# Batched fp32 matmul on one core: loads and stores in one queue, word transposes, full-width matmuls

## The chip, the cores and the metric

The kernel runs on one core of a Trainium2 chip. The metric is device microseconds (us) of one execution, 13 of them for the kernel before. One further execution was taken by the hardware profiler; durations, waits and transfers below come from that one.

## The reference

128 independent products (8 by 16), each of a 256x512 and a 512x384 matrix, in fp32:

```python
b1, b2, m, k, n = 8, 16, 256, 512, 384
return np.matmul(x, weight).astype(np.float32)    # (8, 16, 256, 384)
```

Read are 67.1 MB of `x` and 100.7 MB of `weight`, written are 50.3 MB of output. The kernel casts both inputs to bf16 and sums in fp32.

## The kernel before

One group is two of the 128 matrices (`groups`: 63 pairs, then two single matrices that share one load of `x`). For a group:

- `load_x` (L60) brings the 512 rows of `x` of two matrices, 1 MB, as four consecutive rows per partition, 8 KB in one piece. Partitions 0 to 63 hold the first matrix, 64 to 127 the second. `load_w` (L67) brings one weight matrix, 768 KB, four consecutive rows of K per partition, 6 KB in one piece. Both are issued by SP, in the order x, w, w.
- VectorE (DVE) casts `x` to bf16 in one instruction (L77) and each weight matrix in one (L110).
- TensorE (PE) transposes `x` in 16 blocks of 128x128 bf16 (L82), eight into one PSUM tile; DVE copies each of the two tiles to `x_t` (L86). As the weight rows lie four to a partition, a block takes every fourth column of K (`ko::KO`).
- PE multiplies (L124). A stationary operand is 64 columns of `x_t`, one matrix, so the two matrices of a pair fill the two halves of the output partitions with 32 matmuls of 64 columns by 384. In the two single groups 128 columns are used and 16 matmuls do for one matrix.
- ScalarE (ACT) copies each PSUM tile, 128x768, to `out_sb` (L131), two for a group, and issues the store (L95), 768 KB with 6 KB in one piece per partition. The last two stores are 384 KB with 3 KB per partition.

The code asks for a store three groups late (`LAG`), but the order that the scheduler writes out, and the trace, have each store on ACT's queue right behind its own group's second copy: the first group's copies start at 13.31 and 15.28 us and its store is issued at 16.12 us.

SP's queue has only loads. Buffers: `x_sb` 3, `w_sb` 6, `x_bf` 2, `x_t` 2, `w_bf` 4, `out_sb` 6, PSUM tiles 2 for transposes and 3 for products. Completion counters of transfers are reused in turn, eight in all for loads and stores, four to a group; so each transfer also waits until the one that had its counter, two groups before, has landed.

Of the kernel before, what the change touches and what calls it, by code (L numbers as in the profile page):

```python
# [1 line left out]

# [5 lines left out]


@with_exitstack
def kernel(
    ctx: ExitStack,
    tc: tile.TileContext,
    x: bass.AP,
    weight: bass.AP,
    out: bass.AP,
):
    nc = tc.nc
    P = 128  # L20

    b1, b2, M, K = x.shape
    _, _, _, N = weight.shape
    B = b1 * b2
    KO = K // P

    x_rows = x.rearrange("b1 b2 m k -> (b1 b2 m) k")
    o_rows = out.rearrange("b1 b2 m n -> (b1 b2 m) n")
    w_flat = weight.rearrange("b1 b2 k n -> (b1 b2) k n")

    fp32 = mybir.dt.float32
    bf16 = mybir.dt.bfloat16

    GX = 2
    CX = P // GX
    R = GX * M // P


    groups = [2] * ((B - GX) // 2) + [1] * GX

    LAG = 3

    const = ctx.enter_context(tc.tile_pool(name="const", bufs=1))
    x_pool = ctx.enter_context(tc.tile_pool(name="x_pool", bufs=3))
    xb_pool = ctx.enter_context(tc.tile_pool(name="xb_pool", bufs=2))
    xt_pool = ctx.enter_context(tc.tile_pool(name="xt_pool", bufs=2))
    w_pool = ctx.enter_context(tc.tile_pool(name="w_pool", bufs=6))
    wb_pool = ctx.enter_context(tc.tile_pool(name="wb_pool", bufs=4))  # L50
    out_pool = ctx.enter_context(tc.tile_pool(name="out_pool", bufs=LAG + 3))
    psum_t = ctx.enter_context(tc.tile_pool(name="psum_t", bufs=2, space=bass.MemoryType.PSUM))
    psum_o = ctx.enter_context(tc.tile_pool(name="psum_o", bufs=3, space=bass.MemoryType.PSUM))

    identity = const.tile([P, P], bf16)
    make_identity(nc, identity)

    def load_x(b):
        x_sb = x_pool.tile([P, R, K], fp32, name="x_sb")
        nc.sync.dma_start(  # L60
            x_sb[:], x_rows[b * M : (b + GX) * M].rearrange("(p r) k -> p r k", r=R)
        )
        return x_sb

    def load_w(b):
        w_sb = w_pool.tile([P, KO, N], fp32, name="w_sb")
        nc.sync.dma_start(w_sb[:], w_flat[b].rearrange("(kp ko) n -> kp ko n", ko=KO))  # L67
        return w_sb

    def transpose_x(x_sb, RG):  # L70


        H = R // RG
        x_bf = xb_pool.tile([P, R, K], bf16, name="x_bf")
        x_t = xt_pool.tile([P, RG, KO, P, H], bf16, name="x_t")
        for r0 in range(0, R, 4):
            nc.vector.tensor_copy(out=x_bf[:, r0 : r0 + 4], in_=x_sb[:, r0 : r0 + 4])  # L77
            for r in range(r0, r0 + 4, 2):
                pt = psum_t.tile([P, 2, KO, P], bf16, name="pt")
                for rr in range(2):  # L80
                    for ko in range(KO):
                        nc.tensor.transpose(  # L82
                            pt[:, rr, ko, :], x_bf[:, r + rr, ko::KO], identity
                        )
                j = r % RG
                nc.vector.tensor_copy(  # L86
                    out=x_t[:, j : j + 2, :, :, r // RG], in_=pt[:]
                )
        return x_t

    waiting = []

    def store():
        dram, out_sb = waiting.pop(0)
        nc.scalar.dma_start(out=dram, in_=out_sb)  # L95

    b = 0
    for n, G in enumerate(groups):
        last = n == len(groups) - 1
        C = P // G  # L100
        RG = G * M // P
        if b % GX == 0:
            x_sb = load_x(b)
        w_sb = [load_w(b + i) for i in range(G)]
        if b % GX == 0:
            x_t = transpose_x(x_sb, RG)
        w_bf = []
        for i in range(G):
            t = wb_pool.tile([P, KO, N], bf16, name="w_bf")
            nc.vector.tensor_copy(out=t[:], in_=w_sb[i][:])  # L110
            w_bf.append(t)
        if last:
            while waiting:
                store()

        out_full = out_pool.tile([P, 2 * M // P, N], fp32, name="out_sb")
        out_sb = out_full[:, :RG]
        for r in range(0, RG, 2):
            po = psum_o.tile([P, 2, 512], fp32, name="po")
            for rr in range(2):  # L120
                for ko in range(KO):
                    for i in range(G):
                        c0 = (b % GX + i) * CX
                        nc.tensor.matmul(  # L124
                            po[i * C : (i + 1) * C, rr, :N],
                            x_t[:, r + rr, ko, c0 : c0 + CX, :],
                            w_bf[i][:, ko, :],
                            start=(ko == 0),
                            stop=(ko == KO - 1),
                        )  # L130
            nc.scalar.copy(out=out_sb[:, r : r + 2, :], in_=po[:, :, :N])  # L131
        waiting.append(
            (
                o_rows[b * M : (b + G) * M].rearrange("(p r) n -> p r n", r=RG),
                out_sb,
            )
        )
        if len(waiting) > LAG or last:
            store()
        b += G  # L140


# [1 line left out]
_INS = ['x', 'weight']  # L144
_OUTS = [((8, 16, 256, 384), 'float32')]


# [23 lines left out]
```

## Time and profile before

| | |
|---|---|
| median of 13 runs | 531.51 us (530.08 to 534.75) |
| the profiled execution | 530.08 us |
| its span, first to last instruction | 527.9 us |
| TensorE clock granted, mean | 0.863 |
| busy: PE / DVE / ACT | 342.1 / 277.8 / 103.9 us |
| moved by DMA | 218.59 MB, mean 414 GB/s |

The profiled execution's own time is 2.2 us above its span. "Share" of DMA is the mean busy share of 16 DMA engines; a store or a load is cut over all 16, and counts as landed when the last of them is done. A group passes every 8.1 us (casts of `x` from 5.6 to 515.7 us, 63 steps).

### The profile page before, as it was taken

To read this page: it belongs to the slowest core of one execution; us is meant where nothing else is said; L and a number is where in the kernel's file an instruction comes from. 1 tells how busy PE (TensorE), PEld (TensorE's weight loads), DVE (VectorE), ACT (ScalarE), POOL (GpSimd) and SP (SyncE) were. 2 spreads that over 40 slices of the span, in tenths; PEclk is the share of its full clock that TensorE was granted. 3 is DMA by queue.
4 is the path that set the end of the run, shared out by engine and by line. 5 is a ranking of instruction groups with operands and counts; after the bars stand their busy time and mean duration, and the time that the engine had idled before them with its cause. 6 is when DMAs were issued, how large, how long until landed. Compare 5 with 4: busy or idle time off the path is not lost.

```text
span 527.9 us, 7363 instructions
## 1 busy us (share of the span) xinstructions
PE 342.1 (65%) x3056; PEld 233.1 (44%) x3056; DVE 277.8 (53%) x320; ACT 103.9 (20%) x129; POOL 0.7 (0%) x6
## 2 busy tenths in 40 slices
PE   4685566675764766676657577566676575766764
PEld 2454444444543544444435444344344443544442
DVE  4545545555465544564554545555555555455554
ACT  0212211221211212122112122121111221212212
POOL 0000000000000000000000000000000000000000
PEclk9969888888789878889888878898778988788889
DMA  8999999999999999999999999999999999999994
GB/s 343 405 426 423 425 420 420 425 419 424 422 420 425 421 421 425 421 423 421 423 423 421 421 423 421 423 424 424 422 421 422 422 421 423 421 423 423 424 413 194
DMA packets 37041, 218.59 MB, mean 414 GB/s; under 512 B 4112, under 2 KB 4112, under 8 KB 28816
## 3 DMA queue, kind: packets, MB, share of 16 engines
q1 hardware_dynamic: 27648, 167.78, 76.5%
q10 hardware_dynamic: 9360, 50.34, 23.0%
q8 instruction: 24, 0.39, 0.3%
q14 instruction: 9, 0.07, 0.0%
HBM read 167.77 MB, written 50.33 MB: 413 GB/s over the span
## 4 chain that ended last, share of the span: by engine, by line
DMA 97%; DVE 1%; PE 1%; issue 1%; SPq 0%; ACT 0%; DVEq 0%
DMA x_sb<-in_x_dram 97%; PE po L124 1%; DVE x_t L86 0%; DVE x_bf L77 0%; DVE w_bf L110 0%; SPq L60 0%; SPq L67 0%; ACT out_sb L131 0%; PE pt L82 0%; DVEq L77 0%
## 5 line engine op out<-in xcount | busy, mean ns | idle before, releaser
L124 PE MATMUL po<-w_bf,x_t 128*64 128x384 bf16 (+1 forms) x2032 | 274.7, 405 | 165.0 <-DVE w_bf L110 164.5
L124 PEld LDWEIGHTS <-x_t 128*64 128x64 bf16 (+1 forms) x2032 | 173.0, 134 | 250.9 <-DVE w_bf L110 126.5
L131 ACT COPY out_sb<-po 128x768 f32<-128x768 f32 x128 | 102.6, 802 | 420.0 <-PE po L124 412.5
L77 DVE CAST x_bf<-x_sb 128x2048 bf16<-128x2048 f32 x64 | 78.5, 1227 | 138.8 <-DMA x_sb<-in_x_dram 138.8
L110 DVE CAST w_bf<-w_sb 128x1536 bf16<-128x1536 f32 x128 | 119.9, 955 | 26.9 <-DMA w_sb<-in_weight_dram 26.3
L86 DVE COPY x_t<-pt 128x1024 bf16<-128x1024 bf16 x128 | 83.7, 696 | 78.6 <-PE pt L82 78.6
L82 PE MATMUL pt<-identity,x_bf 128*128 128x128 bf16 x1024 | 70.3, 222 | 16.7 <-DVE x_bf L77 16.7
L82 PEld LDWEIGHTS <-x_bf 128*128 128x128 bf16 x1024 | 60.2, 115 | 39.4 <-DVE x_bf L77 31.0
L131 ACT ACT_TABLE_LOAD x1 | 1.3, 1283 | 0.7 <-PEq L155 0.7
masks.py:199 POOL TENSOR_SCALAR_AFFINE_SELECT identity<-identity 128x128 bf16<-128x128 bf16 x1 | 0.3, 292 | 0.1
masks.py:197 POOL MEMSET identity<- 128x128 bf16 x1 | 0.2, 205 | 0.3 <-POOLq L155 0.3
L155 POOL MEMSET const-bfloat16-1.0<- 128x1 bf16 x1 | 0.1, 101 | 0.0
L155 POOL MEMSET const-uint8-127<- 128x1 uint8 x1 | 0.1, 101 | 0.0
L155 POOL MEMSET const-float32-0.0<- 128x1 f32 x1 | 0.1, 98 | 0.2 <-issue 0.2
L155 POOL MEMSET const-float32-1.0<- 128x1 f32 x1 | 0.1, 98 | 0.0
## 6 DMA issues: line engine op xcount, KB each, us to landing
w_sb<-in_weight_dram SPq DMA_DIRECT2D x128, 768.0 KB, 16.1
x_sb<-in_x_dram SPq DMA_DIRECT2D x64, 1024.0 KB, 16.0
out_dram<-out_sb ACTq DMA_DIRECT2D x63, 768.0 KB, 8.4
out_dram<-out_sb ACTq DMA_DIRECT2D x2, 384.0 KB, 2.3
```

The source lines that it names most:

```text
L77: nc.vector.tensor_copy(out=x_bf[:, r0 : r0 + 4], in_=x_sb[:, r0 : r0 + 4])
L82: nc.tensor.transpose(pt[:, rr, ko, :], x_bf[:, r + rr, ko::KO], identity)
L86: nc.vector.tensor_copy(out=x_t[:, j : j + 2, :, :, r // RG], in_=pt[:])
L110: nc.vector.tensor_copy(out=t[:], in_=w_sb[i][:])
L124: nc.tensor.matmul(po[i * C : (i + 1) * C, rr, :N], x_t[:, r + rr, ko, c0 : c0 + CX, :], w_bf[i][:, ko, :], start=(ko == 0), stop=(ko == K ...
L131: nc.scalar.copy(out=out_sb[:, r : r + 2, :], in_=po[:, :, :N])
L155: nc = _bacc.Bacc("TRN2", target_bir_lowering=False, num_devices=1)
```

## The change

- `nc.sync` (SP) issues stores as well as loads. The store of group n-4 stands behind the loads of group n; behind the loads of the last group stand the four stores still kept back.
- `x_bf` is read as 128x256 fp32 words, each a pair of neighbouring bf16 values. PE transposes words: 8 blocks of 128x128 fp32 for a group, not 16 of bf16. The PSUM tile is read back as bf16 by two DVE copies for a group. In `x_t` the two members of a pair lie side by side, and a stationary operand takes every second element.
- All groups are pairs (64). A matmul uses 128 columns of one matrix: 8 for each matrix, 16 for a group.
- A PSUM tile then holds one matrix on 128 partitions, while `out_sb` holds it on 64 with four rows each. ACT copies it in two halves of 64 partitions, four copies for a group.
- The last group is stored in two halves, each 64 partitions with 6 KB per partition, 384 KB.
- `LAG` is 4, `out_sb` has 7 buffers, the identity is fp32.

```diff
-    identity = const.tile([P, P], bf16)
+    identity = const.tile([P, P], fp32)
...
-        x_t = xt_pool.tile([P, RG, KO, P, H], bf16, name="x_t")
+        x_t = xt_pool.tile([P, J, KO // 2, G, G, C, 2], bf16, name="x_t")
+        words = x_bf[:].bitcast(fp32)
...
-                pt = psum_t.tile([P, 2, KO, P], bf16, name="pt")
+                pt = psum_t.tile([P, 2, KO // 2, P], fp32, name="pt")
                 for rr in range(2):
-                    for ko in range(KO):
+                    for h in range(KO // 2):
                         nc.tensor.transpose(
-                            pt[:, rr, ko, :], x_bf[:, r + rr, ko::KO], identity
+                            pt[:, rr, h, :], words[:, r + rr, h :: KO // 2], identity
                         )
-                j = r % RG
+                j, g = divmod(r, G)
                 nc.vector.tensor_copy(
-                    out=x_t[:, j : j + 2, :, :, r // RG], in_=pt[:]
+                    out=x_t[:, j, :, :, g : g + 2].rearrange(
+                        "k h i g c e -> k g (h i) (c e)"
+                    ),
+                    in_=pt[:].bitcast(bf16).rearrange(
+                        "k g h (i ce) -> k g (h i) ce", i=G
+                    ),
                 )
...
-        nc.scalar.dma_start(out=dram, in_=out_sb)
+        nc.sync.dma_start(out=dram, in_=out_sb)
...
+    for b in range(0, B, G):
+        last = b == B - G
+        x_sb = load_x(b)
+        w_sb = [load_w(b + i) for i in range(G)]
         if last:
             while waiting:
                 store()
+        x_t = transpose_x(x_sb)
+        out_sb = out_pool.tile([P, R, N], fp32, name="out_sb")
+        for i in range(G):
+            w_bf = wb_pool.tile([P, KO, N], bf16, name="w_bf")
+            nc.vector.tensor_copy(out=w_bf[:], in_=w_sb[i][:])
+            po = psum_o.tile([P, J, 512], fp32, name="po")
+            for j in range(J):
                 for ko in range(KO):
+                    nc.tensor.matmul(
+                        po[:, j, :N],
+                        x_t[:, j, ko // 2, i, :, :, ko % 2].rearrange("k g c -> k (g c)"),
+                        w_bf[:, ko, :],
+                        start=(ko == 0),
+                        stop=(ko == KO - 1),
+                    )
+            mine = slice(i * C, (i + 1) * C)
+            for g in range(G):
+                nc.scalar.copy(out=out_sb[mine, g::G, :], in_=po[g * C : (g + 1) * C, :, :N])
+            if last:
+                waiting.append((o_rows[(b + i) * M : (b + i + 1) * M].rearrange(
+                    "(p r) n -> p r n", r=R), out_sb[mine]))
+                store()
+        if not last:
+            waiting.append(
+                (o_rows[b * M : (b + G) * M].rearrange("(p r) n -> p r n", r=R), out_sb[:])
+            )
+            if len(waiting) > LAG:
+                store()
```

## The prediction

> **What bounds the kernel now.** I read the page first: slices, DMA queues, chain.
>
> ```profile
> span 527.9 us, 7363 instructions
> ...
> DMA  8999999999999999999999999999999999999994
> GB/s 343 405 426 423 425 420 420 425 419 424 422 420 425 421 421 425 421 423 421 423 423 421 421 423 421 423 424 424 422 421 422 422 421 423 421 423 423 424 413 194
> ...
> q1 hardware_dynamic: 27648, 167.78, 76.5%
> q10 hardware_dynamic: 9360, 50.34, 23.0%
> q8 instruction: 24, 0.39, 0.3%
> ...
> DMA 97%; DVE 1%; PE 1%; issue 1%; SPq 0%; ACT 0%; DVEq 0%
> ```
>
> The 16 DMA engines are full from the second slice to the last but one, and the chain is 97% transfers. Loads (q1) and stores (q10) have one price: 167.78 MB in 76.5% of the span and 50.34 MB in 23.0% are both 415 GB/s. No engine's work shows until the end. Next the waits of SP, which show how far ahead loads run:
>
> ```profile
> SPq L67 <- DMA w_sb<-in_weight_dram: 253.3, 123, 4.6
> SPq L60 <- DMA x_sb<-in_x_dram: 173.9, 61, 4.0
> ```
>
> Nearly every load waits only for the load two groups before it to land; two groups, 16 us, are always under way. Then busy time by stretches, the last column GB/s and the one before it the DMA share:
>
> ```profile
> 4.00:12.00 8.00, 4.40 (x28) 2.96 (x30) 4.39 (x6) 0.00 (x0) 0.00 (x0) 1.00 1.00 422
> 16.00:24.00 8.00, 4.52 (x53) 3.28 (x50) 5.72 (x8) 1.69 (x3) 0.00 (x0) 1.00 1.01 389
> 50.00:500.00 450.00, 296.94 (x2668) 202.77 (x2668) 238.83 (x276) 88.87 (x111) 0.00 (x0) 0.86 1.02 422
> 514.00:522.00 8.00, 4.80 (x52) 3.58 (x52) 5.44 (x6) 1.60 (x2) 0.00 (x0) 1.00 0.61 249
> 522.00:525.00 3.00, 1.82 (x12) 0.88 (x9) 0.08 (x1) 1.60 (x2) 0.00 (x0) 1.00 0.27 108
> 525.00:528.00 3.00, 0.00 (x0) 0.00 (x0) 0.00 (x0) 0.00 (x0) 0.00 (x0) 0.75 0.40 157
> ```
>
> Loads alone (4 to 12 us) and loads mixed with stores (50 to 500) both run at 422 GB/s. What is lost is lost in the last 14 us. The queues of that window and its timeline say how:
>
> ```profile
> q10 hardware_dynamic: 533, 2.11, 37.5%
> q1 hardware_dynamic: 126, 0.66, 11.4%
> ```
>
> ```profile
> 517.71 0.34 ACTq L95 DMA_DIRECT2D out_dram<-out_sb  x1
> 520.05 2.02 DVE L110 CAST w_bf<-w_sb 128x1536 bf16<-128x1536 f32 x2
> 521.04 2.77 PE L124 MATMUL po<-w_bf,x_t 128*128 128x384 bf16 x16 [2.95 <-DVE w_bf L110]
> 524.68 0.34 ACTq L95 DMA_DIRECT2D out_dram<-out_sb  x1
> ```
>
> At 514 us only 0.66 MB of loads is missing, 1.6 us of work for 16 engines, yet the last weight load (issued at 504.91, 16.1 us to landing) lands at 521.0. 0.66 MB in 7 us is 94 GB/s, what 3.6 engines move at 26.4 each (422/16): some engines lag behind the others, and the slowest sets every landing. It then lands the store issued at 517.71 (5.2 us, 522.9), is idle until the last matrix is computed, and moves the two half stores, landed at 527.0.
>
> **What the Trainium skill says.** Runtime: NRT & Kernel Launch, Instruction fetch mechanics: instructions come by DMA in blocks of 16 KiB, 256 instructions. The trace agrees: PE's 3056 matmuls and 3056 weight loads are 23.9 blocks, q8 has 24 packets. It calls the cost mostly hidden; here one costs a DMA engine 1.06 us (0.3% of 16 x 527.9, over 24). DMA: Bandwidth & Descriptors, Issuing engines are not separate DMA queues: all queues run on the same 16 engines, so moving a store to SP adds no capacity; the two shares above sum to 99.5%, which agrees. SBUF — State Buffer, Door 1: The DMA port swizzle: 64 partitions reach half of the ports. No transfer of this trace uses 64 partitions.
>
> **The change part by part.** The sum is made for the slowest DMA engine, against the span.
>
> *Stores kept back, SP's order.* Before, the slowest engine is busy up to 522.9 us with all but the last two half stores, 0.786 MB, 0.049 MB for each engine, 1.86 us at 26.4 GB/s. After, the ring behind the last load holds four whole stores (4 x 1.86 = 7.4 us) and then the halves, without a pause, if the last group is computed in time: 522.9 + 1.86 = 524.8, about 0.3 for the receipt (my estimate, from 2.3 us to landing less 0.34 issue and 0.93 of moving, most of it start), and the 0.96 us that lie between the last landing and the end: 526.0. Gain **1.9**.
>
> *Is it computed in time?* The last load lands at 524.8 - 1.86 - 7.4 = 515.5. Then one cast 0.96, 8 matmuls (half of the 2.77 above) 1.4, two ACT copies of 0.80 each, issue 0.34, about 1 to start: 520.8. The ring is busy until 522.9. Cover 2.1 us; each us beyond it costs one.
>
> *Does a store block the loads behind it on SP?* Loads n+1 stand behind store n-4. That store waits for ACT's copies of group n-4. Loads n go when x of n-2 has landed; a group's copies end 8 to 9 us after its x (509.0 to 517.7 for the group before the last), and group n-4's x landed 16 us earlier. Spare 7 us, so nothing; if not, each us of it stops all loads. Each store puts 0.34 us of issue on SP, 1.4 us of four issues per 8.1 us. ACT loses those issues.
>
> *Fewer instructions.* PE falls from 95.5 a group to 8 transposes plus 16 matmuls with 16 weight loads, 40 (48 if a word transpose counts twice): 2560 to 3072, 10 to 12 blocks, not 24. Some 13 x 1.06 = 14 us of engine time go. Spread over 16 engines it is 0.9 on each; all on four, as the 3.6 above hints, 3.5. I take **2.2**, both ends kept.
>
> *Half stores on 64 partitions.* If 16 engines share half of the ports, each costs 0.93 more: 0 to 1.9. The slowest engine reads last, when others are done: **-0.3**.
>
> *Direction order in one ring.* Both mixes move 422 above, so 0; I keep 1%, 5 us, to both sides.
>
> *The engines.* Edits at nothing, covered by the 8.1 us that a group's transfers take. PE: 16 full-width matmuls 2.8 at full clock, 3.2 at 0.86; half as many transposes, but of fp32 words: no such row. Below, the price of the bf16 ones (16 in 1.08, so 0.54 for 8; fewer can't cost more), above, four times it, 2.2. TensorE: Matmul & The Clock Gate, Terms, says a transpose mode makes fp32 4 times faster, which speaks for the lower half; no run shows it. Between the two PE waits for `x_t`, 0.65 to 2.5 (two copies, 1.24 each when strided). Worst: 2.2 + 2.5 + 3.2 = 7.9. DVE: 1.23 + 2 x 0.96 + 2 x (0.65 to 1.24) = 4.4 to 5.6. ACT: four copies on 64 partitions, at 0.80 each as before by elements per partition, 3.2. Without the cover all PE time above 8.1 counts 64 times.
>
> Sum: 1.9 + 2.2 - 0.3 = **3.8 us**, span 524.1, the profiled execution 526.3. The runs' median is 1.4 above the profiled execution; taken from it, **527.7 us**.
>
> **Rivals.**
>
> *One ring runs better (0.12).* The lag of some engines may come from two rings taken in turn: 16 to 24 us, where the first store starts (issued at 16.12), moves 389, not 422, 0.6 us lost. Against: the rate is 422 with and without stores. With 1%: 527.7 - 5 = 522.7.
>
> *Hidden anyway (0.14).* Fetches spread evenly (0.9) and half the ports bind (-1.9): 1.9 + 0.9 - 1.9 = 0.9, 530.6. For it: nothing names the lagging engines' work. Same if the changed order did nothing; but in the compiled program each store does stand behind the loads four groups later.
>
> *One ring runs worse (0.08, the other side).* A descriptor of the other direction waits behind its predecessor in the same ring, where two rings let the engine take the other: at every change of direction, twice a group and engine, something drains. It decides from 3.8/128 = 0.03 us for each change; at 0.1 us it costs 12.8: 540. For it: no stretch shows both directions in one ring. Against: loads of different tiles follow without a gap, share 1.00.
>
> *PE becomes the bound (0.04).* Word transposes above (8.1 - 2.5 - 3.2)/8 = 0.30 us each with slow copies, 0.50 with quick ones. At 0.6: 4.8 + 1.3 + 3.2 = 9.3 a group, 64 of them, 595.
>
> **How the numbers follow.** The forecast has 0.62 and covers gains of 2 to 6, 525.5 to 529.5. Rivals as above. A measurement of this kernel tells 0.3%, 1.6 us, from no change. Faster: 0.62 + 0.12 = 0.74; same 0.14; slower 0.08 + 0.04 = 0.12. The range 522 to 531.5 holds the forecast, "hidden" and most of "better", and leaves out the slower cases.
>
> **What would show it.** Right: the last weight load lands near 513 to 516, DMA share stays above 0.9 until 3 us before the end, q8 has 10 to 12 packets, 422 GB/s in the middle, only small waits of SP for ACT. Wrong: a middle below 419 or above 426 (ring), DMA below 0.95 there with PE or DVE in the chain (engines), a pause between the fourth store and the halves (compute too late), halves of over 1.5 us (ports).

## The result

| | before | after |
|---|---|---|
| median of the runs, us | 531.94 (48 runs, 530.07 to 534.75 and one of 658.13) | 526.37 (11 runs, 525.77 to 526.90) |
| ratio, 95% interval | | 0.9892, 0.9876 to 0.9908 |
| profiled execution / its span, us | 530.08 / 527.9 | 526.52 / 524.5 |
| TensorE clock granted | 0.863 | 0.845 |
| busy PE / DVE / ACT, us | 342.1 / 277.8 / 103.9 | 328.2 / 272.8 / 204.5 |

The change makes the kernel 1.1% faster. Forecast were 527.7 us and a range of 522 to 531.5. The medians differ by 5.6 us, the two spans by only 3.4: the profiled execution before was one of its fastest, the one after is near the middle of its runs.

The page of the changed kernel, slices, DMA queues and chain:

```profile
span 524.5 us, 4635 instructions
...
DMA  8999999999999999999999999999999999999996
GB/s 340 422 417 424 422 423 420 424 424 419 424 424 420 423 421 422 424 422 422 426 420 424 422 424 422 421 425 426 422 426 423 422 424 425 424 423 424 425 424 247
...
q1 hardware_dynamic: 36880, 218.12, 100.1%
q8 instruction: 12, 0.20, 0.1%
...
DMA 97%; issue 1%; ACT 1%; SPq 0%; ACTq 0%
```

One queue carries everything, the rate of the middle is as before, and q8 has 12 packets where it had 24: PE issues 1536 matmuls and 1536 weight loads, so each word transpose has its own weight load. The chain is still 97% transfers. The last two slices moved 413 and 194 GB/s before, 424 and 247 now.

Busy time by stretches (last columns: PE clock, DMA share, GB/s):

```profile
16.00:24.00 8.00, 5.35 (x33) 3.38 (x33) 5.82 (x7) 3.18 (x4) 0.00 (x0) 1.00 1.01 416
50.00:500.00 450.00, 287.07 (x1335) 164.18 (x1335) 237.45 (x279) 174.60 (x221) 0.00 (x0) 0.83 1.01 423
514.00:516.00 2.00, 2.00 (x9) 1.04 (x10) 1.41 (x2) 0.00 (x0) 0.00 (x0) 0.70 0.88 366
516.00:519.00 3.00, 1.33 (x9) 0.59 (x6) 0.00 (x0) 2.84 (x4) 0.00 (x0) 1.00 0.48 190
519.00:522.00 3.00, 0.00 (x0) 0.00 (x0) 0.00 (x0) 0.34 (x1) 0.00 (x0) 1.00 1.02 250
```

From 516 to 519 us the DMA engines work for 0.48 of the time: some are out of work while the last group is computed, the others, which lag, are still moving kept-back stores. The trace has 16 landing times for a transfer, which I read as one for each engine. Those of the fourth kept-back store run from 515.4 to 519.4 us for fifteen of them; the sixteenth is at 521.6. The timeline and the stores of that stretch:

```profile
514.46 0.95 DVE L113 CAST w_bf<-w_sb 128x1536 bf16<-128x1536 f32 x1
516.12 3.22 ACT L126 COPY out_sb<-po 64x768 f32<-64x768 f32 x4 [5.45 <-issue]
```

```profile
L99 SPq DMA_DIRECT2D out_dram<-out_sb x1: 332/332/332, 510.7 to 510.7; - x1
DMA to landing us min/median/max: 10.9/10.9/10.9
...
L99 SPq DMA_DIRECT2D out_dram<-out_sb x1: 466/466/466, 519.4 to 519.4; - x1
DMA to landing us min/median/max: 4.1/4.1/4.1
```

The last weight load lands at 514.1 (521.0 before) and its cast starts at 514.46. The fourth kept-back store lands at 510.7 + 10.9 = 521.6, and the last half, issued at 519.4, at 523.5. Between 519.4 and 521.6 the slowest engine still had other work. Of these 2.2 us the issue takes 0.5 and the start about 1, as the prediction estimates it, so compute was hidden with some 0.8 us to spare.

### The profile page after: what moved, and what is told of

The parts are those of the page before. It is cut to its first block, busy times and chain, and to the rows that moved or that the text cites. A ratio compares the mean times of both kernels' runs of the same rounds, so it can differ in the third digit from the quotient of the medians.

```text
span 524.5 us, 4635 instructions
## 1 busy us (share of the span) xinstructions
PE 328.2 (63%) x1536; PEld 188.9 (36%) x1536; DVE 272.8 (52%) x320; ACT 204.5 (39%) x257; POOL 0.7 (0%) x6
## 4 chain that ended last, share of the span: by engine, by line
DMA 97%; issue 1%; ACT 1%; SPq 0%; ACTq 0%
DMA w_sb<-in_weight_dram 93%; DMA x_sb<-in_x_dram 3%; ACT out_sb L126 1%; ACTq L162 0%; SPq L66 0%; SPq L59 0%
## 5 line engine op out<-in xcount | busy, mean ns | idle before, releaser
L126 ACT COPY out_sb<-po 64x768 f32<-64x768 f32 x256 | 203.2, 794 | 314.1 <-issue 273.0
L117 PE MATMUL po<-w_bf,x_t 128*128 128x384 bf16 x1024 | 235.1, 393 | 46.8 <-DVE x_t L85 36.9
L81 PE MATMUL pt<-identity,x_bf 128*128 128x128 f32 x512 | 93.3, 338 | 142.3 <-DVE x_bf L76 142.2
L117 PEld LDWEIGHTS <-x_t 128*128 128x128 bf16 x1024 | 110.8, 115 | 163.5 <-DVE x_t L85 59.7
L113 DVE CAST w_bf<-w_sb 128x1536 bf16<-128x1536 f32 x128 | 121.9, 955 | 38.4 <-DMA w_sb<-in_weight_dram 38.4
L81 PEld LDWEIGHTS pt<-identity,x_bf 128*128 128x128 f32 x512 | 78.0, 213 | 164.6 <-issue 160.9
```

What stands on the lines that cost most here:

```text
L81: nc.tensor.transpose(pt[:, rr, h, :], words[:, r + rr, h :: KO // 2], identity)
L113: nc.vector.tensor_copy(out=w_bf[:], in_=w_sb[i][:])
L117: nc.tensor.matmul(po[:, j, :N], x_t[:, j, ko // 2, i, :, :, ko % 2].rearrange("k g c -> k (g c)"), w_bf[:, ko, :], start=(ko == 0), stop= ...
L126: nc.scalar.copy(out=out_sb[mine, g::G, :], in_=po[g * C : (g + 1) * C, :, :N])
```

## The experiments

The theory at the start: kept-back stores hide the last group's compute (1.9 us), and fewer instruction blocks relieve the slowest DMA engine (1.3 us, from 522.9 to 521.6 for all but the last halves). Rivals: the single queue does everything, or the leaner compute does.

**The queue alone.** Compute as before; in `store()` and ahead of the last group:

```diff
-    LAG = 3
+    LAG = 4
...
-        nc.scalar.dma_start(out=dram, in_=out_sb)
+        nc.sync.dma_start(out=dram, in_=out_sb)
```

(and the flush of kept-back stores stands behind the last loads)

> The kernel before with its compute, only the stores moved to SP, four groups behind their loads. Theory (the gain is stores kept back, about 1.9 us, plus fewer instruction blocks, about 1.3): 24 blocks stay, so 1.9 us under the kernel before: median about 530.0 against 531.9. Rival one (the single queue with its fixed order does all of it, and also takes the scatter of the runs away): 526 to 527. Rival two (the leaner compute does all of it): 532, no change.

Measured: 526.14 us (526.02 to 526.50), ratio 0.9891, 0.9874 to 0.9907. All of the gain, with 24 blocks and the old compute: rival one. Its timeline and a stretch near the end:

```profile
515.15 4.05 PE L123 MATMUL po<-w_bf,x_t 128*128 128x384 bf16 x16 [2.95 <-DVE w_bf L113]
515.46 0.96 DVE L113 CAST w_bf<-w_sb 128x1536 bf16<-128x1536 f32 x1 [0.36 <-DMA w_sb<-in_weight_dram]
```

```profile
516.00:519.00 3.00, 3.00 (x12) 1.21 (x10) 0.42 (x1) 0.80 (x1) 0.00 (x0) 0.59 0.72 298
```

The same 16 matmuls that took 2.77 us at the end of the kernel before take 4.05 here, at a mean clock of 0.67 against 1.00. (They are the two single groups, 8 matmuls each; the description of the kernel before wrongly gives 16 to one matrix.) Little is lost, for DMA works on through them at a share of 0.72, and the last store is issued at 520.1 us, before the slowest engine is done with the kept-back ones at 521.0.

**The compute alone.** The changed kernel with the stores back on ACT:

```diff
-        nc.sync.dma_start(out=dram, in_=out_sb)
+        nc.scalar.dma_start(out=dram, in_=out_sb)
```

> The changed kernel with only the stores given back to ACT, each right behind its own group's copies as before. Theory: 12 blocks in place of 24 are worth about 1.3 us, the pause before the last stores is back: about 530.6. Rival one (the queue does all): 532, scatter as before, 530 to 535. Rival two (compute does all): 526.4.

Measured: 531.82 (531.14 to 533.73), ratio 0.9998, 0.9982 to 1.0015: nothing on balance, though q8 has 12 packets. End of its timeline and two stretches:

```profile
519.57 0.96 DVE L113 CAST w_bf<-w_sb 128x1536 bf16<-128x1536 f32 x1 [0.34 <-DMA w_sb<-in_weight_dram]
525.91 0.48 ACTq L99 DMA_DIRECT2D out_dram<-out_sb  x1
```

```profile
519.00:522.00 3.00, 2.71 (x9) 1.35 (x10) 1.20 (x2) 0.00 (x0) 0.00 (x0) 0.50 0.11 47
525.00:528.00 3.00, 0.00 (x0) 0.00 (x0) 0.00 (x0) 0.87 (x2) 0.00 (x0) 0.62 0.84 180
```

From the last cast to the last store are 6.3 us (521.1 to 524.68, 3.6, before): PE's 16 matmuls take 4.24 us, at a mean clock of 0.64, and four copies stand in place of two. DMA stands nearly still meanwhile, its share 0.11. The last half then takes 3.5 us to land where it took 2.3: 180 GB/s at a share of 0.84 is 214 for a full share, against 157 at 0.40, 393, before. So the changed compute lengthens an end that isn't hidden, and this run is no price of fetches alone: all but the last halves had landed at 521.4 us, 1.5 earlier than before, and the longer end took that back.

**Two stores kept back, not four.** `LAG = 2` in the changed kernel.

> The changed kernel with two stores kept back in place of four: the store of group n-2 stands behind the loads of group n. Theory (the kept-back stores are the work that hides the last group's compute): the last load lands 3.7 us later, two stores of 3.7 us lie behind it and compute takes 5.0, so DMA pauses and the last half lands 2 to 3.5 us later: 528.3 to 530. Rival (one queue in itself is the gain, whatever is kept back): 526.4 within 0.5.

Measured: 529.59 (528.88 to 530.53), ratio 0.9958, 0.9942 to 0.9974, inside what the theory said. One queue is not enough; 3.2 of the 5.6 us go when two stores fewer lie behind the last load. (No run keeps four stores back on ACT's queue; what the second queue by itself does is tried below with transfers alone.) Its stretch of the pause:

```profile
519.00:522.00 3.00, 2.37 (x14) 1.12 (x11) 0.28 (x1) 1.81 (x3) 0.00 (x0) 0.94 0.07 29
```

**Six stores kept back.** `LAG = 6`, nine output buffers.

> The changed kernel with six stores kept back and two more output buffers. The last half was issued at 519.4 and the slowest engine busy until 521.6, a cover of 2.2 us; more cover can't shorten what the slowest engine has to move: 526.4 within 0.3. If the last group's compute still sets the end in most runs: 525 or less, since its 1.9 us less of late loads would show.

Measured: 526.23 (525.88 to 526.50), ratio 0.9886, 0.9870 to 0.9903: no more is to be had. Four suffice.

**One store for the last group**, 128 partitions:

```diff
-            if last:
-                waiting.append((... out_sb[mine]))
-                store()
-        if not last:
-            waiting.append((..., out_sb[:]))
-            if len(waiting) > LAG:
-                store()
+        waiting.append((..., out_sb[:]))
+        if last or len(waiting) > LAG:
+            store()
```

> The changed kernel with its last group stored in one piece of 128 partitions in place of two halves of 64[...], but it can't start before the second matrix is copied. Theory (the slowest engine still has kept-back stores when the halves come, so their half rate is hidden): 526.4 within 0.3. Rival (the half rate, 250 GB/s at a full DMA share, is paid): 525.4 or less.

Measured: 526.13 (525.92 to 526.58), ratio 0.9886, 0.9869 to 0.9903. The half rate of halves is real (214 GB/s for a full share in the compute alone, above) and hidden: 0.24 us lie within the scatter of the runs.

**Instruction blocks: padding.** Ahead of each matrix's matmuls in the changed kernel:

```diff
+            for _ in range(12):
+                nc.tensor.matmul(po[:32, 0, N : N + 8], x_t[:, 0, 0, i, 0, :32, 0],
+                                 w_bf[:, 0, :8], start=True, stop=True)
```

> The changed kernel with 24 small weight loads and 24 small matmuls more in each group (32 columns by 8, results unused), so that PE has as many instructions as before: 24 blocks to fetch in place of 12. PE's own time rises by some 2 us a group, which transfers of 8.1 us cover. Theory: the slowest DMA engine has 0.8 (spread evenly) to 3.2 (four engines) us more work, 527.2 to 529.6 against 526.4. Rival (instruction fetches don't matter): 526.4 within 0.3.

Measured: 528.10 (527.46 to 529.42), ratio 0.9929, 0.9912 to 0.9946; 1.7 us more, in the middle of the theory's span. But its timeline shows a second reason:

```profile
517.53 2.74 PE L125 MATMUL po<-w_bf,x_t 128*128 128x384 bf16 x8
520.31 1.60 ACT L134 COPY out_sb<-po 64x768 f32<-64x768 f32 x2 [1.44 <-PE po L125]
```

The last copies end at 521.9, not 519.3, so the last half came late in this execution. So the cover was raised as well, padding with `LAG = 6` and nine buffers:

> The padded kernel of before (PE with as many instructions as the kernel before) with six stores kept back in place of four and two more output buffers. Theory (padding cost 1.7 us because the last group's compute outgrew the kept-back stores): cover grows by 3.7 us and the cost goes: 526.4. Rival (padding costs by its fetches): 528.1 as before.

Measured: 528.34 (527.82 to 528.56), ratio 0.9929, 0.9905 to 0.9952. That is 2.1 us more than six stores without padding (526.23). More cover didn't help: the last kept-back store itself lands at 523.7 us, 521.6 without padding. Late compute isn't what costs here; fetches or the padding itself are, and no run separates these two.

**Transfers alone.** No compute at all, the changed kernel's loads and stores:

```diff
-        x_t = transpose_x(x_sb)
-        out_sb = out_pool.tile([P, R, N], fp32, name="out_sb")
...
-            nc.scalar.copy(out=out_sb[mine, g::G, :], in_=po[g * C : (g + 1) * C, :, :N])
+        out_sb = fixed      # one tile of zeros
```

> The changed kernel's loads and stores in the same order on SP and nothing else: no cast, transpose, matmul or copy; every store writes one tile of zeros, so the output is zeros. No instruction blocks are fetched for PE. If the lag of the slowest DMA engine comes from fetches alone: the floor of evenly loaded engines, 2.2 to start, 13.63 MB per engine at 26.45 GB/s 515.3, about 1 to the end: span 518.5, time 520.6. If the lag has another cause in the transfers themselves: a span of 522 to 524 as in the changed kernel less about 1, time 524 to 526.

Measured: 523.45 (522.72 to 523.75), ratio 0.9836, 0.9817 to 0.9855; between the two expectations. The floor of this order of transfers is 2.9 us below the changed kernel.

**Transfers with stores on ACT's queue:**

```diff
+        out_sb = fixed[(b // G) % 7]      # seven tiles of zeros
         for i in range(G):
...
+            nc.vector.tensor_copy(out=out_sb[:, i, 0:1], in_=w_sb[i][:, 0, 0:1])
+        nc.scalar.dma_start(out=..., in_=out_sb[:])
```

> Transfers alone again, but stores on ACT's queue, each issued as soon as its own group's weights have landed (VectorE writes two columns of the stored tile from them, nothing else is computed; the output is not the product). Against transfers alone on SP's queue, 523.45. Theory one (two rings in themselves make DMA engines drift apart): span of landings and scatter of the runs as in the kernel before, 3 us or more between the runs, median 526 to 529. Theory two (the rings are equal, only the order at the end counts): the last store can't be hidden, 1.6 us: 525.0, scatter within 1 us.

Measured: 524.54 (524.47 to 524.75), ratio 0.9861, 0.9837 to 0.9884. Nearer to theory two. Two rings as such bring no scatter (0.3 us) and little drift: the 16 landings of the last weight load spread over 3.6 us, against 2.2 on one ring and 8.9 in the kernel before. The 1.1 us more than one ring are less than the 1.6 at which an unhidden last store was priced.

**Transfers with instruction blocks.** Small matmuls on PE, 48 and then 24 pairs a group:

```diff
+        few = xb_pool.tile([P, 40], bf16, name="few")
+        nc.vector.tensor_copy(out=few[:], in_=x_sb[:, 0, :40])
...
+        for _ in range(48):
+            nc.tensor.matmul(po[:32, 0, :8], few[:, :32], few[:, 32:], start=True, stop=True)
```

> Transfers alone on SP's queue plus 48 small weight loads and 48 small matmuls in each group (from 40 cast columns of x, results unused; the output is zeros), so 24 instruction blocks are fetched as in the kernel before, with hardly any operand traffic. Theory (fetches are nearly free, as the unpadded against padded landing of the fourth kept store showed, 521.6 and 521.8): 523.4 to 524.0. Rival (the fetches make the lag of the slowest engine): 525 to 527.

> Transfers alone on SP's queue plus 24 small weight loads and 24 small matmuls in each group (output zeros, results unused): 12 blocks. Between 523.45 with none and 526.98 with 24. If each block costs the same: 525.2. If the engines are hit in turn, eight blocks to a round, two rounds for the unlucky: about 525.0 to 525.9.

Measured: 526.98 (526.64 to 527.18) with 24 blocks, 526.09 (525.47 to 526.45) with 12, 523.45 with none: the first 12 cost 2.6 us, the next 0.9. Ratios 0.9906 (0.9884 to 0.9927) and 0.9882 (0.9863 to 0.9902). With 24 the rival was right; 12 cost more than either expectation, so blocks don't cost the same each. Part of the first 2.6 us isn't by block: in the profiled executions, from 24 to 48 us, where one block is fetched, the kernel with 12 moved 407 GB/s, the one without 420, the one with 24 417, some 0.7 us lost once (24 x 13/420). The step from none to 12 also brings the cast and PE's small matmuls; no run has these without their fetches. The three kernels' stretch from 519 to 522 us, without blocks, with 12, with 24 (busy columns of DVE and POOL; then of PE, PEld, DVE and POOL):

```profile
519.00:522.00 3.00, 0.00 (x0) 0.00 (x0) 1.00 0.04 18
```

```profile
519.00:522.00 3.00, 0.00 (x0) 0.00 (x0) 0.00 (x0) 0.00 (x0) 1.00 0.41 170
```

```profile
519.00:522.00 3.00, 0.00 (x0) 0.00 (x0) 0.00 (x0) 0.00 (x0) 1.00 0.56 233
```

What remains late is a part of the engines. Of the 16 landings of the last weight load the first and the last are 2.2 us apart without blocks, 6.3 with 12 and 7.0 with 24. It is 6.0 in the changed kernel, 8.9 before, 5.9 with the queue alone.

**Padding the queue-alone kernel**, 36 blocks, the same 12 matmuls ahead of each PSUM tile:

> The compute of before with the stores on SP, four groups late (526.14 with 24 blocks), plus 24 small weight loads and matmuls in each group as in the padded kernel: 36 blocks. If a block costs 0.15 us on the slowest DMA engine, as padding the changed kernel (12 more, 1.7) and transfers alone (24 more, 3.5) say: 527.9. If this kernel's fetches fall where they cost nothing: 526.2.

Measured: 529.97 (528.71 to 531.29), ratio 0.9954, 0.9937 to 0.9972: more than either expectation. It doesn't settle the price of a block, for its last copy started only at 523.74 us, 4.5 later than without padding (519.29). Of these, 3.0 are a later last weight load (518.3, not 515.4), which fetches may explain and late compute doesn't (from 60 to 490 us SP waits for an engine 0.4 us at most); the rest is padding and PE's clock at the end.

## Why the prediction was right, point by point

**The bound and the order at the end: right, and stores in SP's queue are the whole gain.** The last load was put at 515.5 and landed at 514.1 in the changed kernel and about 515.4 with the queue alone. From there to the start of the last half the prediction had 5.3 us, its issue and start included, with a cover of 2.1; to the issue alone it took 5.3, and counted like the prediction the cover was 0.8. That six stores gain nothing fits the reckoning of 7.4 us of stores over 5.3 of compute. Two stores should lose 1.6 by it (5.3 less 3.7) and lose 3.2: the sign is right, the size is not, and the half rate of the halves, not hidden there, is one reason.

**Its size, 1.9, was too small.** The queue alone took 3.9 us from the span (527.9 to 524.0) and 5.7 from the medians. Two terms failed.

The first is the 522.9 at which all but the last halves land: the order was taken to leave it as it was. With the queue alone it came at 521.0, 1.9 earlier, while the pause itself gave about what was forecast: from there to the last landing are 4.1 us before (to 527.0) and 1.9 after (to 522.9). Of the 1.9, some 0.8 are gained by 500 us, where 210.25 MB have been moved in place of 209.91 (0.34 MB at 422 GB/s). Little of it comes from the start, where the kernel before moves only 389 GB/s from 16 to 24 us: kernels with stores on SP have their own dip later, and from 16 to 48 us the rates are 416 before, 418 with the queue alone and 417 after. The rest, engines that lie less far apart at the end, stays open: all but the last halves is landed at 522.9 before, 521.0 with the queue alone, 521.4 with the compute alone, 521.6 after, an order by neither queues nor blocks.

The second is carrying the pause of one profiled execution, and a fixed 1.4 us to the median, over to the changed kernel. In that execution PE's clock was 1.00 throughout the end and the pause short; with the stores given back to ACT it was 6.3 us from the last cast to the last store, four copies and a clock of 0.64 in the matmuls included. After the change this time is hidden, and the runs lie within 1.1 us of each other, not 4.7. That the clock of the last group makes the scatter of the kernel before fits these traces but is argued, since only one execution of it was traced.

**Fewer instructions, 2.2: wrong.** The step priced 12 or more blocks fewer at 0.9 to 3.5 on the slowest engine. Between the queue alone (24 blocks, 526.14) and the changed kernel (12, 526.37) there is nothing. The upper end took four engines to lag; of the 16 landings of the last weight load before, eight come after 517.5 us. Kernels with more blocks were slower all the same, by 2.6 us for the first twelve beside transfers alone, with what came along, and by 1.7 and 2.1 for twelve in the padded kernels; why the queue-alone kernel doesn't pay for its second twelve is not settled. So two errors, an end sized too small and a gain from fetches that isn't there, partly cancelled. That the forecast came within 1.3 us is luck: without the fetches it would have been 529.9, 3.5 too slow. The Trainium skill (Runtime: NRT & Kernel Launch, Instruction fetch mechanics) calls the cost mostly hidden; in the pair of kernels compared here no cost shows, beside bare transfers 24 blocks and their matmuls cost 3.5 us.

**Half stores, -0.3.** The half rate is there: 214 GB/s for a full share in the compute alone, about half of 422, as Door 1 of the Trainium skill's page SBUF — State Buffer has it, where 64 partitions reach half of the ports. With four stores kept back its cost is 0: whole or in halves, 526.13 and 526.37.

**SP's order.** Nothing waits for ACT in the steady part; SP's waits of the changed kernel:

```profile
SPq L66 <- DMA w_sb<-in_weight_dram: 175.0, 119, 2.2
SPq L59 <- DMA x_sb<-in_x_dram: 120.9, 58, 2.9
SPq L99 <- DMA out_dram<-out_sb: 88.3, 58, 2.9
...
SPq L99 <- ACT out_sb L126: 12.6, 4, 6.6
```

Four waits for ACT, 12.6 us in all: one of 0.4 within the first 60 us, and three, 12.2 in all, after 505 us, for the last kept-back store and the two halves, whose groups were still to be computed. Nearly every other load and store goes when a transfer of two groups before lands.

**The engines.** The groups of the changed kernel:

```profile
L126 ACT COPY out_sb<-po 64x768 f32<-64x768 f32 x256 | 203.2, 794 | 314.1 <-issue 273.0
L117 PE MATMUL po<-w_bf,x_t 128*128 128x384 bf16 x1024 | 235.1, 393 | 46.8 <-DVE x_t L85 36.9
L81 PE MATMUL pt<-identity,x_bf 128*128 128x128 f32 x512 | 93.3, 338 | 142.3 <-DVE x_bf L76 142.2
```

A copy of 64 partitions costs what one of 128 did (794 and 802 ns), so ACT doubled its work unharmed. Eight word transposes take 1.20 us at full clock, inside the bounds of 0.54 and 2.2; `x_t` copies 0.68. All stays hidden in 8.1 us a group.

**The rivals.** One ring better or worse: 423 against 422 GB/s in the middle, and two rings alone cost 1.1 us with an unhidden last store, so neither by the 5 us that were kept for them; the 0.8 us gained by 500 us may still be the ring's or the order's. Hidden anyway: no. PE the bound: no, 1.20 us for eight transposes is 0.15 each. (Its bound with quick copies is 0.45, not 0.50: 8.1 less 1.3 and 3.2, over 8.) What I said would show it held for the last load, q8 and the middle; that DMA would stay above 0.9 until 3 us before the end did not (0.48 from 516 to 519): it overlooked that the quick engines run out first, though the sum was made for the slow ones. Halves of over 1.5 us, named as a sign of being wrong, came (384 KB at 214 GB/s take 1.8) and cost nothing, being hidden.

## What to carry to other kernels

Where transfers bound a kernel, the last tile's compute can still be paid in full, because nothing is left to move: keep back as many finished stores as that compute takes to move, and place them behind the last load in the same queue, where they delay no load. The measure is bytes kept back over the DMA rate against the time from the last landing to the last store at the lowest clock the profile shows. Check in the compiled order that a lag written in the code is there at all; before, each store stood right behind its own group's copies in spite of `LAG = 3`.

## What the runs showed of the hardware that was not expected

One transfer's 16 landings, at most 0.5 us apart at the start, drift apart over 500 us: to 2.2 us in transfers alone, 6.0 in the changed kernel, 8.9 before, and the last of them decides when the transfer has landed. Beside bare transfers, 12 fetches of 16 KB instructions, 0.2 MB in 218, came with 2.6 us more (523.45 to 526.09) and 12 more with 0.9, several times their bytes' share. That only some engines are hit by them fits the drift (2.2, 6.3, 7.0 us) but the traces don't name the engines. How long the last group takes varies with PE's clock: the same 16 matmuls took 2.77 us at 1.00, 4.05 at 0.67 with the queue alone and 4.24 at 0.64 with the compute alone. A pause in DMA makes the kernel pay for that, kept-back stores hide it.
